# A hybrid block on one core: the recurrence's gates as pairs of 64-row matmuls, with the squares and some transposes in other slots

## The chip, the cores and the metric

The kernel runs on one core of one Trainium2 chip. The metric is the device time of one execution in microseconds. PE is TensorE, ACT ScalarE, DVE VectorE, POOL GpSimd, and SP the engine whose queue issues most DMAs.

## The reference

One block of a network over 512 tokens of 1024 features, in fp32: a norm, one input projection into seven parts, a gated linear recurrence and differential attention beside each other, a gated merge, an output projection with residual, a norm, an MLP and a last norm. What the change touches is the recurrence's gates (and the slots of the attention's steps):

```python
def rg_lru(x, w_a, b_a, w_x, b_x, lam):
    bsz, s, _ = x.shape
    xb = x.reshape(bsz, s, RNN_BLOCKS, RNN_BLOCK_W)
    r = jax.nn.sigmoid((jnp.einsum('bsni,nij->bsnj', xb, w_a) + b_a).astype(jnp.float32)).reshape(bsz, s, D_RNN)
    i = jax.nn.sigmoid((jnp.einsum('bsni,nij->bsnj', xb, w_x) + b_x).astype(jnp.float32)).reshape(bsz, s, D_RNN)
    log_a = -LRU_C * r * jax.nn.softplus(-lam.astype(jnp.float32))
    a = jnp.exp(log_a)
    mult = jnp.sqrt(-jnp.expm1(2.0 * log_a))
    u = mult * i * x.astype(jnp.float32)
...
    h = rms_norm(x, norm1_g[l])
    proj = h @ w_in[l]
    u_x, u_g, q, k, v, g_r, g_a = jnp.split(proj, cuts, axis=-1)
    xr = causal_depthwise_conv(u_x, conv_w[l], conv_b[l])
    y_rnn = rg_lru(xr, rg_a_w[l], rg_a_b[l], rg_x_w[l], rg_x_b[l], lru_lambda[l]) * jax.nn.gelu(u_g)
...
    y_attn = diff_attention(q, k, v, lam, lam_init, subln_g[l])
    merged = (jax.nn.sigmoid(g_r) * (y_rnn @ w_br_rnn[l])
              + jax.nn.sigmoid(g_a) * (y_attn @ w_br_attn[l]))
```

RNN_BLOCKS is 16 and RNN_BLOCK_W 64: each gate is sixteen products with a 64x64 matrix. There are 8 heads; a head has two maps of 64 features each.

## The kernel before, in words

Activations lie transposed, features on the 128 partitions and the 512 tokens along the free axis, in 8 tiles. Every fp32 product is split: each operand is a high part (hi, a cast to fp32r on ACT) and a rest (lo, a subtraction on DVE), and a product is three matmuls, hi by hi, hi by lo and lo by hi.

The first stage computes v; the norm's factors follow. The second, to which the change belongs, runs over 32 slots, j = 0 to 3 and n = 0 to 7 with s = 8j + n. Each slot issues one projection chunk of 24 matmuls of 128x128x512 (L166 to L168, output pmm). By n the chunk is q or k of head 2j (n = 0, 1), u_x (2, 3), q or k of head 2j + 1 (4, 5) or u_g (6, 7). Behind the chunk come the steps that `at(slot, f)` has placed there. For each head these are the scores in two halves (L544, pairs of matmuls of 64 rows; softmax on DVE and ACT, exponentials at L346), three groups of transposes of the probabilities (L582, copied out by ACT at L587 into pT or tmp), the product with v (`attn_out`, L598, copied out by ACT at L601 into Q) and the sums of squares of its output (`o_squares`, L608 on ACT). The table `sl` holds the slots of a head's steps, counted from its k chunk. At n = 5 come `lru_gates` and `lru_decay`, behind n = 7 the gelus of u_g, `lru_scan` (a square root on ACT, products and scans on DVE, L678 and L680) and `lru_out` (L683).

`lru_gates(j)` handles 256 features, as two tiles e of 128. For each e it loads a block-diagonal 128x128 matrix for each of the two gates (two 64x64 matrices on the diagonal), splits them (gwh on ACT, L654; gwl on DVE), and issues for each gate three matmuls of 128x128x512 (L659 to L661) into one half of a PSUM tile "sc" and a sigmoid of 128x512. The scores use the same two "sc" buffers.

The scheduler of the language decides the order of the instructions of each engine, within the dependences and the order in which the program is written. `act` chains the activations that need a table in the order of the program; `tc.keep_in_program_order` holds an instruction behind the one issued before it. `raw` are weights on arrival, `whi` and `wlo` their split (L136 and L137 by chunk, L204 and L205 by piece of the later units).

The third stage goes through units: "gr" (gate of the recurrence branch, sigmoid L346 into up or rot), "rnn" (branch matmuls on E and L), "ga", "att", "out", and the MLP's "one" and "two" (matmuls at L249). The last heads' scores, transposes, outputs and squares run between the first "gr" chunks, from slot 32 on.

Of the kernel before, what the change touches and what calls it, by code (L numbers as in the profile page):

```python
# [8 lines left out]
F = mybir.dt.float32  # L9
# [5 lines left out]
P = 128  # L15
# [5 lines left out]
NH = 8  # L21
# [275 lines left out]
def block_kernel(ctx: ExitStack, tc: tile.TileContext, a):  # L297
# [57 lines left out]
    def col(off, i):  # L355
        return sm[:, off + i:off + i + 1]
# [287 lines left out]
    def lru_gates(j):  # L644
        r_, i_, xr = lru_st[j][:3]
        xh_, xl_ = t("L3", (P, 2, T), FR), t(f"R{j}", (P, 2, T), FR)
        A.copy(xh_, xr)
        V.tensor_tensor(xl_, xr, xh_.bitcast(F), op=ALU.subtract)
        for e in range(2):
            m = 2 * j + e  # L650
            gw = t("tmp", (P, 2, P), bufs=2)
            nc.sync.dma_start(gw, a["gates"][m])
            gh, gl = t("gwh", (P, 2, P), FR), t("gwl", (P, 2, P), FR)
            A.copy(gh, gw)  # L654
            V.tensor_tensor(gl, gw, gh.bitcast(F), op=ALU.subtract)
            pgs = ps("sc", (P, 2, T), bufs=2)
            for g, dst, boff in ((0, r_, C_AB), (1, i_, C_XB)):
                pg = pgs[:, g]
                TE.matmul(pg, gh[:, g], xh_[:, e], start=True, stop=False)  # L659
                TE.matmul(pg, gh[:, g], xl_[:, e], start=False, stop=False)  # L660
                TE.matmul(pg, gl[:, g], xh_[:, e], start=False, stop=True)  # L661
                act(dst[:, e], pg, AF.Sigmoid, bias=col(boff, m))
        lru_st[j][3] = t("L3", (P, 2, T))

    def lru_decay(j):
# [28 lines left out]
    for j in range(KT // 2):  # L694
        for n in range(8):
            s = 8 * j + n
            p_ = b.proj(xh, xl)
            h = 2 * j + n // 4
            if n % 4 < 2:
                if n % 4 == 0:  # L700
                    qk = t(f"B{h % 2}", (P, 2, T))
                rope_load(p_, qk, n % 4)
                if n % 4 == 1:
                    qks = rope(h, qk)


                    sl = ((3, 6, 5, 8, 9, 10, 13), (4, 5, 6, 7, 8, 9, 12))[h % 2]
                    if h == NH - 1:
                        sl = (3, 4, 5, 6, 7, 8, 11)
                    for d, f, *args in zip(sl[2:], (attn_transpose,) * 3 + (attn_out, o_squares),  # L710
                                           (h,) * 5, ((0, 1), (2,), (3,), None, h + 1)):
                        at(s + d, f, *(x for x in args if x is not None))
                    at(s + sl[0], attn_scores, h, qks, 0)
                    at(s + sl[1], attn_scores, h, qks, 2)
            elif n < 4:
                lru_conv(j, n - 2, p_)
                if n == 3:
                    at(s + 2, lru_gates, j)
                    at(s + 2, lru_decay, j)
            else:  # L720
                if n == 6:
                    p_g = p_
                else:
                    yr[j] = t(f"R{j}", (P, 2, T))
                    act(yr[j][:, 0], p_g, AF.Gelu_apprx_tanh)
                    act(yr[j][:, 1], p_, AF.Gelu_apprx_tanh)
                    lru_scan(j)
                    lru_out(j)
            run(s)
# [239 lines left out]
def _layout(inputs):  # L969
# [20 lines left out]
        cols(g["rg_a_b"][0].reshape(-1)), cols(g["rg_x_b"][0].reshape(-1)), cols(g["lru_lambda"][0]),  # L990
        cols(g["conv_w"][0].reshape(-1)), cols(g["subln_g"][0]),
    ], axis=1)
    gates = np.zeros((KT, P, 2, P), np.float32)
    for s, n in ((0, "rg_a_w"), (1, "rg_x_w")):
        for blk in range(16):
            o = (blk % 2) * 64
            gates[blk // 2, o:o + 64, s, o:o + 64] = g[n][0, blk]
    half = HD // 2
    inv = np.float32(ROPE_THETA) ** (-np.arange(half, dtype=np.float32) * np.float32(2.0) / np.float32(HD))
    ang = np.arange(T, dtype=np.float32)[None, :] * inv[:, None].astype(np.float32)  # L1000
# [38 lines left out]
```

## Time and profile before

| | |
|---|---|
| median of 3 runs | 882.9 us (882.69 to 883.09) |
| profiled execution | 881.29 us, its span 879.5 us |
| granted TensorE clock, mean | 0.997 |
| busy PE, weight load, DVE, ACT | 867.0, 742.4, 623.1, 495.0 us |
| chain that ended last | PE 92%, ACT 3%, DVE 3% |

The table comes from the page of the profile: the busy time of an engine is the sum of its instructions, its share an average over all stages. The chain is followed back from the last instruction to what released it.

### The profile page before, as it was taken

The numbers are of one execution on the slowest core, as the hardware profiler recorded it, in microseconds if no ns is written. First come the engines' busy times: TensorE is split into PE (matmuls) and PEld (weight loads), VectorE is DVE, ScalarE is ACT, GpSimd is POOL, SyncE is SP. The second block draws the span as 40 slices with busy tenths as digits, with TensorE's granted clock in tenths as the row PEclk, the third lists the DMA queues.
The fourth block names the chain that finished last, engine by engine and source line by source line (L and its number), as shares of the span: only waits on it lengthen the run. The fifth ranks groups of instructions, "written<-read, shape, count | busy, mean of one in ns | idle before, by whom it ended". The sixth has DMA issues, their size and how long they took to land.

```text
span 879.5 us, 13019 instructions
## 1 busy us (share of the span) xinstructions
PE 867.0 (99%) x5033; PEld 742.4 (84%) x5033; DVE 623.1 (71%) x1071; ACT 495.0 (56%) x925; POOL 11.0 (1%) x17
## 2 busy tenths in 40 slices
PE   9999999999999999999999999999999999999996
PEld 7887788788788788889888889988888888888996
DVE  7777787795986866677765997766666666665533
ACT  7544856957868974544443555644444444444532
POOL 0000000000000012000000000000000000000000
PEclk9999999999999999999999999999999999999998
DMA  8433223134232257223225221222222222222211
GB/s 299 143 138 115 72 78 128 59 108 132 72 109 72 63 166 209 66 97 132 107 102 188 97 96 48 97 99 98 102 103 104 105 104 102 97 96 97 97 49 48
DMA packets 23917, 94.40 MB, mean 107 GB/s; under 512 B 3376, under 2 KB 6704, under 8 KB 14896
## 3 DMA queue, kind: packets, MB, share of 16 engines
q1 hardware_dynamic: 22128, 90.43, 29.7%
q0 software_dynamic: 1728, 3.15, 2.1%
q8 instruction: 39, 0.64, 0.3%
q14 instruction: 22, 0.18, 0.1%
HBM read 83.08 MB, written 2.10 MB: 97 GB/s over the span
## 4 chain that ended last, share of the span: by engine, by line
PE 92%; ACT 3%; DVE 3%; DMA 1%; issue 1%; SPq 0%; POOL 0%; DVEq 0%; ACTq 0%
PE pmm L249 38%; PE psc L249 22%; PE pmm L166 7%; PE pmm L167 7%; PE pmm L168 7%; PE pmm L454 3%; PE psc L454 3%; PE pmm L598 2%; PE psc L544 2%; DMA S<-X 1%; PE ptr L582 1%; ACT L346 1%; ACT L L346 1%; PE psc L659 0%; PE ptr L385 0%
## 5 line engine op out<-in xcount | busy, mean ns | idle before, releaser
L204 ACT CAST whi<-raw 128x512 fp32r<-128x512 f32 (+1 forms) x236 | 144.2, 627 | 207.5 <-PE pmm L249 103.9
L205 DVE TENSOR_TENSOR wlo<-raw,whi 128x512 fp32r<-128x512 f32 (+1 forms) x236 | 162.3, 697 | 48.0 <-ACT whi L204 44.7
L249 PE MATMUL psc<-X,whi 128*128 128x256 f32 x592 | 112.3, 288 | 0.6 <-DVE up L273 0.2
L249 PEld LDWEIGHTS psc<-X,whi 128*128 128x128 f32 x592 | 91.8, 189 | 8.1 <-DVE up L273 1.7
L249 PE MATMUL pmm<-E,whi 128*128 128x512 f32 x256 | 82.2, 397 | 0.3 <-ACT rot L346 0.3
L249 PE MATMUL psc<-X,wlo 128*128 128x256 f32 x296 | 81.1, 281 | 0.0
L166 PE MATMUL pmm<-X,whi 128*128 128x512 f32 x200 | 81.0, 405 | 0.0
L249 PE MATMUL pmm<-L,whi 128*128 128x512 f32 x256 | 80.6, 396 | 0.0
L167 PE MATMUL pmm<-X,whi 128*128 128x512 f32 x200 | 79.3, 397 | 0.0
L168 PE MATMUL pmm<-X,wlo 128*128 128x512 f32 x200 | 79.3, 396 | 0.0
L249 PE MATMUL psc<-Q,whi 128*128 128x256 f32 x320 | 70.2, 287 | 0.8 <-DVE tmp L269 0.8
L249 PEld LDWEIGHTS psc<-Q,whi 128*128 128x128 f32 x320 | 52.3, 188 | 6.4 <-DVE tmp L269 3.2
L249 PEld LDWEIGHTS pmm<-L,whi 128*128 128x128 f32 x256 | 48.1, 188 | 11.3
L249 PE MATMUL pmm<-B,whi 128*128 128x512 f32 (+1 forms) x224 | 57.6, 346 | 0.0
L249 PEld LDWEIGHTS pmm<-E,whi 128*128 128x128 f32 x256 | 47.7, 189 | 9.7 <-ACT rot L346 0.5
L249 PEld LDWEIGHTS psc<-X,wlo 128*128 128x128 f32 x296 | 55.0, 189 | 0.0
L249 PE MATMUL pmm<-V,whi 128*128 128x512 f32 (+1 forms) x192 | 53.2, 357 | 0.0
L249 PE MATMUL pmm<-L,wlo 128*128 128x512 f32 x128 | 50.8, 397 | 0.0
L249 PE MATMUL pmm<-E,wlo 128*128 128x512 f32 x128 | 50.7, 396 | 0.0
L136 ACT CAST whi<-raw 128x1024 fp32r<-128x1024 f32 (+1 forms) x36 | 34.3, 955 | 27.4 <-PE pmm L167 22.0
L166 PEld LDWEIGHTS pmm<-X,whi 128*128 128x128 f32 x200 | 37.7, 189 | 10.4 <-issue 1.5
L137 DVE TENSOR_TENSOR wlo<-raw,whi 128x1024 fp32r<-128x1024 f32 (+1 forms) x36 | 39.3, 1099 | 8.8 <-ACT whi L136 8.8
(312 smaller groups left out, 1873.5 us busy)
## 6 DMA issues: line engine op xcount, KB each, us to landing
raw<-wts SPq DMA_DIRECT2D x70, 1024.0 KB, 4.8
rot<-B SPq DMA_DIRECT2D x64, 64.0 KB, 2.0
L<-xT SPq DMA_DIRECT2D x8, 256.0 KB, 5.3
raw<-wts SPq DMA_DIRECT2D x8, 256.0 KB, 5.3
S<-X SPq DMA_DIRECT2D x8, 256.0 KB, 2.8
S<-X POOLq DMA_DIRECT2D x8, 256.0 KB, 4.4
R<-xT SPq DMA_DIRECT2D x8, 256.0 KB, 4.6
out<-R SPq DMA_DIRECT2D x6, 256.0 KB, 2.5
```

Source lines behind the costliest of these rows:

```text
L136: nc.scalar.copy(hf[:, s], raw[:, s])
L137: nc.vector.tensor_tensor(lf[:, s], raw[:, s], hf[:, s].bitcast(F), op=ALU.subtract)
L166: nc.tensor.matmul(ps, hi[:, k], xh[k], start=(k == 0), stop=False)
L167: nc.tensor.matmul(ps, hi[:, k], xl[k], start=False, stop=False)
L168: nc.tensor.matmul(ps, lo[:, k], xh[k], start=False, stop=(k == KT - 1))
L204: self.nc.scalar.copy(hi, src)
L205: self.nc.vector.tensor_tensor(lo, src, hi.bitcast(F), op=ALU.subtract)
L249: nc.tensor.matmul(out, l[:, k], r, start=((first if clear is None else clear) and k == 0 and g == 0), stop=(last and k == 3 and g == 2), ...
L346: ins = A.activation(*args, **kw).ins
L454: TE.matmul(pvs[half][i], xs[q][:, i * P:(i + 1) * P], (hv, lv)[wi][:, q % 2], start=(q == 0 and n == 0), stop=(q == KT - 1 and n == 2))
L544: ins = TE.matmul(scs[i - i0][:, m, :n], l[rows, 0, i * P:n], r[rows, 1, :n], start=(g == 0), stop=(g == len(terms_) - 1))
L598: TE.matmul(po[:, i], pdT[:, j], v[j][:, h * P:(h + 1) * P], start=(j == 0), stop=(j == i))
```

## The change

It does four things. (1) The gates of one j are one transfer and one split instead of two: the host lays the matrices out so that the 64 rows of a 64x64 block hold both gates' matrices side by side, 64 columns each. (2) The matmuls use 64 rows each: for each e and each of the three products a pair, one on the upper and one on the lower half of the rows, each with 128 columns of which 64 belong to each gate; both e follow one another without another matmul between, and hold both "sc" buffers. Twelve matmuls per j, as before. (3) The result of a pair's half c has one gate on partitions 0 to 63 and the other on 64 to 127, the other way round for c = 1. So the sigmoids take 64 rows each: eight of 64x512 for each j in place of four of 128x512; those of the second gate read from one half of the partitions and write to the other. (4) In the table of slots the squares of the even heads come one slot earlier and those of the odd ones two later; for heads 4 to 6 they come at slots 33 to 35. An odd head's first transposes and second group come one slot later.

```diff
+        gw = t("tmp", (P, 2, P), bufs=2)
+        nc.sync.dma_start(gw, a["gates"][j])
+        gh, gl = t("gwh", (P, 2, P), FR), t("gwl", (P, 2, P), FR)
+        A.copy(gh, gw)
+        V.tensor_tensor(gl, gw, gh.bitcast(F), op=ALU.subtract)
+        pgs = [ps("sc", (P, 2, T), bufs=2) for _ in range(2)]
+        first = True
         for e in range(2):
-            m = 2 * j + e
-            gw = t("tmp", (P, 2, P), bufs=2)
-            nc.sync.dma_start(gw, a["gates"][m])
-            gh, gl = t("gwh", (P, 2, P), FR), t("gwl", (P, 2, P), FR)
-            A.copy(gh, gw)
-            V.tensor_tensor(gl, gw, gh.bitcast(F), op=ALU.subtract)
-            pgs = ps("sc", (P, 2, T), bufs=2)
-            for g, dst, boff in ((0, r_, C_AB), (1, i_, C_XB)):
-                pg = pgs[:, g]
-                TE.matmul(pg, gh[:, g], xh_[:, e], start=True, stop=False)
-                TE.matmul(pg, gh[:, g], xl_[:, e], start=False, stop=False)
-                TE.matmul(pg, gl[:, g], xh_[:, e], start=False, stop=True)
-                act(dst[:, e], pg, AF.Sigmoid, bias=col(boff, m))
+            for g, (l, r) in enumerate(((gh, xh_), (gh, xl_), (gl, xh_))):
+                for c in range(2):
+                    rows = slice(c * HD, (c + 1) * HD)
+                    ins = TE.matmul(pgs[e][:, c], l[rows, e], r[rows, e], start=(g == 0), stop=(g == 2))
+                    if not first:
+                        tc.keep_in_program_order(ins)
+                    first = False
+        for e in range(2):
+            for dst, boff, flip in ((r_, C_AB, 0), (i_, C_XB, 1)):
+                for c in range(2):
+                    to, of = (slice(x * HD, (x + 1) * HD) for x in (c, c ^ flip))
+                    act(dst[to, e], pgs[e][of, c], AF.Sigmoid, bias=col(boff, 2 * j + e)[to])
...
-                    sl = ((3, 6, 5, 8, 9, 10, 13), (4, 5, 6, 7, 8, 9, 12))[h % 2]
+                    sl = ((3, 6, 5, 8, 9, 10, 12), (4, 5, 7, 8, 8, 9, 14))[h % 2]
                     if h == NH - 1:
                         sl = (3, 4, 5, 6, 7, 8, 11)
+                    if 4 <= h < NH - 1:
+
+                        sl = sl[:6] + (8 * NH // 2 + h - 3 - s,)
...
-    gates = np.zeros((KT, P, 2, P), np.float32)
+    gates = np.zeros((KT // 2, P, 2, 2, HD), np.float32)
     for s, n in ((0, "rg_a_w"), (1, "rg_x_w")):
         for blk in range(16):
             o = (blk % 2) * 64
-            gates[blk // 2, o:o + 64, s, o:o + 64] = g[n][0, blk]
+            gates[blk // 4, o:o + 64, blk // 2 % 2, s ^ (blk % 2)] = g[n][0, blk]
+    gates = gates.reshape(KT // 2, P, 2, P)
```

The order on ACT in the second block of gates (j = 1), before. `gwh` is the cast of the gates' matrices, `psc` the gates' PSUM, `L` the gates r and i, `S` the split of head 3's q and k, `Q` the output of a head; the squares are the L608 rows:

```order
L136 CAST whi_1436<-raw_1378 128x1024
L654 CAST gwh_1357<-tmp_1355 128x256
L346 ACTIVATE L_203_1112<-psc_1346,small_61 128x512
L524 CAST S_243_1325<-B_227_1242 128x1024
L346 ACTIVATE L_202_1111<-psc_1361,small_61 128x512
L608 ACTIVATE tmp_1410,ss_544<-Q_220_1203,r_101_543 128x128
L608 ACTIVATE tmp_1412,ss_544<-Q_220_1203,r_101_543 128x128
L608 ACTIVATE tmp_1414,ss_544<-Q_220_1203,r_101_543 128x128
L346 ACTIVATE L_203_1112<-psc_1361,small_61 128x512
L346 ACT_TABLE_LOAD
L346 ACTIVATE L_257_1370<-L_202_1111,cneg_536 128x512
```

The same place after the change:

```order
L136 CAST whi_1432<-raw_1383 128x1024
L652 CAST gwh_1349<-tmp_1347 128x256
L524 CAST S_239_1318<-B_222_1234 128x1024
L346 ACT_TABLE_LOAD
L346 ACTIVATE L_199_1109<-psc_1353,small_61 64x512 x2
L346 ACTIVATE L_200_1110<-psc_1353,small_61 64x512 x2
L346 ACTIVATE L_199_1109<-psc_1354,small_61 64x512 x2
L346 ACTIVATE L_200_1110<-psc_1354,small_61 64x512 x2
L346 ACT_TABLE_LOAD
L346 ACTIVATE L_255_1375<-L_199_1109,cneg_536 128x512
L601 COPY Q_217_1201<-pmm_1414 128x512
```

All sigmoids of the block now stand behind the cast of S and the table load, and the squares are gone from between them.

The order on PE where the last heads' steps end and the first branch matmuls begin, before. `ptr` are transposes of probabilities, V the values, pT and tmp the copied transposes, E the operand of the branch matmuls; the place is behind the last "gr" chunk:

```order
L598 MATMUL pmm_2866<-V_39_137,pT_2542 128x128
L598 MATMUL pmm_2866<-V_37_135,tmp_2827 128x128
L598 MATMUL pmm_2866<-V_38_136,tmp_2827 128x128
L598 MATMUL pmm_2866<-V_39_137,tmp_2827 128x128
L598 MATMUL pmm_2866<-V_40_138,tmp_2827 128x128
L582 MATMUL ptr_2879<-ident_108,B_535_2777 128x128 x3
L598 MATMUL pmm_2891<-V_37_135,pT_2833 128x128 x2
L598 MATMUL pmm_2891<-V_38_136,pT_2833 128x128
L249 MATMUL pmm_2930<-E_515_2686,whi_2390 128x512 x2
L249 MATMUL pmm_2930<-E_515_2686,wlo_2391 128x512
L249 MATMUL pmm_2930<-E_516_2689,whi_2390 128x512
L582 MATMUL ptr_2884<-ident_108,B_535_2777 128x128 x4
```

The same place after the change:

```order
L598 MATMUL pmm_2858<-V_39_137,pT_2525 128x128
L582 MATMUL ptr_2821<-ident_108,B_495_2657 128x128 x3
L598 MATMUL pmm_2858<-V_37_135,tmp_2819 128x128
L598 MATMUL pmm_2858<-V_38_136,tmp_2819 128x128
L598 MATMUL pmm_2858<-V_39_137,tmp_2819 128x128
L598 MATMUL pmm_2858<-V_40_138,tmp_2819 128x128
L582 MATMUL ptr_2880<-ident_108,B_519_2760 128x128 x3
L598 MATMUL pmm_2892<-V_37_135,pT_2825 128x128 x2
L598 MATMUL pmm_2892<-V_38_136,pT_2825 128x128
L249 MATMUL pmm_2922<-E_499_2669,whi_2379 128x512 x2
L582 MATMUL ptr_2885<-ident_108,B_519_2760 128x128 x4
```

The last head's first transposes (`ptr_2821`) have come out of the last "gr" chunk to this place, and two branch matmuls in place of four stand ahead of its last transposes.

## Rows read from the trace of the kernel before

**Rows 1.** The page, part 1: busy time, share of the span and instructions.
```profile
PE 867.0 (99%) x5033; PEld 742.4 (84%) x5033; DVE 623.1 (71%) x1071; ACT 495.0 (56%) x925; POOL 11.0 (1%) x17
```

**Rows 2.** Busy time in windows: PE, PEld, DVE, ACT, POOL; clock; DMA.
```profile
280.00:300.00 20.00, 19.32 (x99) 14.17 (x99) 17.35 (x34) 19.14 (x37) 0.00 (x0) 1.00 0.03 10
300.00:320.00 20.00, 19.54 (x111) 16.22 (x110) 11.07 (x21) 19.85 (x52) 3.65 (x4) 1.00 0.74 207
```

**Rows 3.** Timeline of PE, first block: start, duration, engine, line, operation.
```profile
90.32 0.50 PE L659 MATMUL psc<-L,gwh 128*128 128x512 f32 x1
90.65 0.39 PE L660 MATMUL psc<-R,gwh 128*128 128x512 f32 x1
```

**Rows 4.** Timeline of PE: pairs of 64-row matmuls of the scores.
```profile
101.15 0.39 PE L168 MATMUL pmm<-X,wlo 128*128 128x512 f32 x1
101.47 0.44 PE L544 MATMUL psc<-E 64*128 64x384 f32 x2
101.75 0.51 PE L544 MATMUL psc<-E,E 64*128 64x384 f32 x4
102.10 0.39 PE L544 MATMUL psc<-E 64*128 64x512 f32 x2
102.33 0.63 PE L544 MATMUL psc<-E,E 64*128 64x512 f32 x4
102.89 0.50 PE L166 MATMUL pmm<-X,whi 128*128 128x512 f32 x1
103.23 0.39 PE L167 MATMUL pmm<-X,whi 128*128 128x512 f32 x1
```

**Rows 5.** Groups by line and form on ACT: the gates' sigmoids (busy, mean ns).
```profile
L346 ACT ACTIVATE L<-psc,small 128x512 f32<-128x512 f32 x16 | 11.0, 686 | 4.3 <-PE psc L661 4.2
```

**Rows 6.** Timeline of ACT, second block; in brackets the idle time ahead.
```profile
151.68 0.41 ACT L654 CAST gwh<-tmp 128x256 fp32r<-128x256 f32 x1
...
153.48 1.05 ACT L524 CAST S<-B 128x1024 fp32r<-128x1024 f32 x1 [0.81 <-DVE B L521]
154.50 0.69 ACT L346 ACTIVATE L<-psc,small 128x512 f32<-128x512 f32 x1
155.09 0.39 ACT L608 ACTIVATE tmp<-Q,r 128x128 f32<-128x128 f32 x1
...
157.06 1.28 ACT L346 ACT_TABLE_LOAD   x1
158.35 0.72 ACT L346 ACTIVATE L<-L,cneg 128x512 f32<-128x512 f32 x1
```

**Rows 7.** Timeline of ACT: an exponential of 128 columns.
```profile
295.54 0.37 ACT L346 ACTIVATE B<-psc,nb 128x128 f32<-128x128 f32 x1
```

**Rows 8.** Timeline of ACT, fourth block.
```profile
269.47 1.14 ACT L204 CAST whi<-raw 128x512 fp32r<-128x512 f32 x2 [1.41 <-PE pmm L167]
...
274.51 0.67 ACT L346 ACTIVATE L<-psc,small 128x512 f32<-128x512 f32 x1
```

**Rows 9.** Timeline of PE, second block: gates, next chunk, transposes of the even head.
```profile
148.01 0.39 PE L659 MATMUL psc<-L,gwh 128*128 128x512 f32 x1
...
162.36 0.50 PE L166 MATMUL pmm<-X,E 128*128 128x512 f32 x1
...
173.57 0.49 PE L582 MATMUL ptr<-ident,B 128*128 128x128 f32 x3
```

**Rows 10.** Timeline of DVE, second block.
```profile
167.03 1.23 DVE L678 TENSOR_TENSOR L<-L,L 128x1024 f32<-128x1024 f32 x1 [1.24 <-ACT L L346]
...
172.28 1.28 DVE L571 SCALAR_TENSOR_TENSOR B<-up,cf,B 128x384 f32<-128x384 f32 x2
```

**Rows 11.** Timeline of ACT, first block: first and last of four sigmoids.
```profile
89.58 0.69 ACT L346 ACTIVATE L<-psc,small 128x512 f32<-128x512 f32 x1
...
94.28 0.69 ACT L346 ACTIVATE L<-psc,small 128x512 f32<-128x512 f32 x1 [1.05 <-PE psc L661]
```

**Rows 12.** Timeline of PE at the first branch matmuls.
```profile
313.44 0.74 PE L249 MATMUL pmm<-E,whi 128*128 128x512 f32 x2 [0.32 <-ACT rot L346]
```

## The prediction

> **What bounds the kernel now.** I read the page first: TensorE (PE) is busy 867.0 of 879.5 us, 99% [rows 1], so at first sight every microsecond of matmul that goes is a microsecond of time. That share is an average, and the change lies in four places (four blocks, one for each j) between 82 and 320 us. So next I read the windows: between 280 and 320 us ScalarE (ACT) is busy 19.14 and 19.85 us of 20, while PE loses 0.68 and 0.46 us [rows 2]. Ahead of the end of this stage ACT has no time left and PE is the one that waits: an ACT chain that gets longer there is paid in full. Then the timelines of PE and ACT around a block say how long the removed matmuls take and who waits for what.
>
> The profiled execution took 881.29 us, a span of 879.5 and 1.79 around it; the median of the three runs is 882.9, so the profile stands 1.6 us (0.18%) under it. I add what follows to the median. A measurement of this kernel can tell about 0.2% from no change, 1.8 us.
>
> **PE: the gates' matmuls.** Before, a block issues twelve 128-row matmuls of 512 columns, one every 0.23 us, and loses time where they follow other shapes: 90.32 to 90.65 is 0.33 instead of 0.23 [rows 3]; all such steps of the first block make 0.41. 12 x 0.229 + 0.41 = 3.16 us. The new form, 64-row pairs that run at the same time, has its model in the scores, which use the same pairs [rows 4]: 102.10 to 102.33 is 0.23 for a pair of 512 columns, as long as one matmul of 128 rows. Entering costs 0.09 (101.15 to 101.47 is 0.32), the first pair 0.10 more than the next (0.28 for 384 columns against half of 0.35), leaving 0.10 (102.33 to 102.89 is 0.56 for two pairs) and the matmul behind it 0.11 (102.89 to 103.23 is 0.34). Six pairs in a row: 6 x 0.23 + 0.38 to 0.40 = **1.76 us**. So PE has less work by 3.16 - 1.76 = 1.40 in block 1; in blocks 2 to 4, where the twelve cost 3.0 to 3.2, by about 1.25 each. Together 5.2 us: the most that the change can give.
>
> The trace shows that pairs cost an entry and an exit. The Trainium skill (TensorEngine Tiling (Array Packing), Key Properties) states that changing the tiling mode drains TensorE, and it agrees; the same page (PSUM Bottleneck) says that tiling speeds up TensorE but not the evacuation of PSUM, and advises to use VectorE too. That is a rule against this change as written, since all eight sigmoids of a block stay on ACT.
>
> **ACT: the sigmoids.** Before, four of 128x512 per block, 686 ns each [rows 5], 0.59 from start to start (154.50 to 155.09 [rows 6]). After, eight of 64x512. The trace has no 64-row instruction on ACT, so I bound its price: below by half, 0.30, if time went with all elements; above by 0.59, the same. An exponential of 128 columns takes 0.37 and the sigmoid of 512 columns 0.69 [rows 6, 7]: time goes with the free size, and that stays 512. I take **0.59**; four more cost 2.36 per block, and one of two casts of the gates (0.41 [rows 6]) goes.
>
> The Trainium skill (ScalarE: Activation LUTs, What ACT_TABLE_LOAD costs) says 280 ns + 0.833 ns per column, one element per cycle in each lane: 706 ns for 512 columns, whatever the rows; the 686 of the trace agree, and no run here shows 64 rows. By it the sum is the same.
>
> More than the 2.36 matters where they stand. Before, the sigmoids were spread among the matmuls, and ACT did the table load and the first of them in its gaps (0.81 idle ahead of 153.48 even so [rows 6]; 1.41 ahead of 269.47 [rows 8]). After, the order shows all eight behind the cast of S, which waits for DVE at 153.48, and behind the table load.
>
> - Block 2 (block 3 repeats it). Cast S 153.48, sigmoid table at 154.50, first sigmoid at 155.78, eight by 0.59 end at 160.6; before, the exp table followed at 157.06 [rows 6]. Chain +3.5; one square (0.39) leaves it: the square root behind it ends at 170.2 instead of 167.0.
> - What this holds up, first: the next chunk takes the PSUM bank of attn_out, so PE waits for the copy of Q. After the sigmoids come table 1.28, one exponential 0.72 [rows 6], the copy, some 0.5: it ends at 163.1. PE started that chunk at 162.36 [rows 9] and, 0.56 faster by the new matmuls (1.25 less the 0.69 below), would want it at 161.8. The gain is gone and 0.7 more.
> - Second: DVE's products and scans of the recurrence start at 167.03 on that square root, and the combination of the softmax (L571) is behind them; its first half ends at 172.9 [rows 10], 5.9 behind the root. PE transposes it at 173.57 [rows 9], with only 0.7 to spare. After: wanted at 163.1 + 11.2 = 174.3, there at 170.2 + 5.9 = 176.1. PE stands **2.5 us** later than before at this place. Of it the three matmuls at 148.01 [rows 9], now behind that chunk, give back 0.69 ahead of it; DVE has one split of gates less ahead of 153.48, for which I take off 0.2. Net **+1.6** each for blocks 2 and 3, +3.2.
> - Block 1: there no cast stands ahead of the sigmoids. The four began at 89.58 and, each waiting for its matmuls, ended at 94.97 [rows 11]; eight in a row from 89.58 end at 94.4. Nothing comes later, so I keep the whole **-1.4**. If the chain came as in block 2, it would be up to +1.6.
> - Block 4: -0.7 for the group ahead of the chunk's end. Then ACT: from 269.47 (a wait for the chunk's end [rows 8]) two casts 1.14, cast of gates 0.4, two squares 0.78, cast S 1.05, table 1.28, eight sigmoids 4.72: 278.8, where the last sigmoid ended at 275.2 before [rows 8]. +3.6. From there to 313 ACT is full but for some 1.0 us [rows 2], of which I let 0.5 be taken up: **+3.1** at the second gate sigmoid, for which PE waited already (0.32 ahead of 313.44 [rows 12]).
> - The end of the stage. The new order has the last head's first transposes behind the last gate chunk, where they were inside it, and on ACT the copies of pT behind two casts and a copy of Q. PE may wait 2.1 us more for them, or, if it finds other work, 0. I take the middle, **+1.0**.
>
> **Edits with one answer.** The gates' four transfers fewer on SP (and their splits on DVE) land long before they are used: nothing. The squares' slots: they change places on ACT, their number is the same; what left blocks 2 and 3 is counted, and in the slots where they go (19, 21, 27) ACT has idle time that hides them; without that cover each 0.39. The odd heads' later first transposes leave PE its number of transposes, and give the softmax a slot (5.5 us) more: counted at 0, below by what they save, the 0.2 to 0.5 us waits of such places; above 0.
>
> **Sum:** -1.4 + 3.2 - 0.7 + 3.1 + 1.0 = +5.2 us: 882.9 + 5.2 = **888.1 us**, slower by 0.6%.
>
> **The rivals.**
> 1. The slack is larger than I count, and ACT bites only in block 4: -1.4 - 2.5 - 0.7 + 3.1 + 0 to 1.0 = -1.5 to -0.5: about 881.9. For it: 0.7 of slack is a small number out of a long chain, and the scheduler has moved the odd heads' transposes too. Against: the head that waits here is the even one, whose slots stay. It decides if the root ends within 0.7 us of its time of before.
> 2. 64-row sigmoids take half the time: eight end 2.4 us earlier, the root stands +0.8 in blocks 2 and 3 and is covered, block 4 pays 1.2 with PE's gain kept ahead: -1.4 - 2.5 - 0.7 + 1.7 = -2.9: 880.0. Against: 0.37 for 128 columns, 0.69 for 512 [rows 6, 7].
> 3. **Faster, the other side:** ACT has no deadline at all in these blocks, because PE, where it waits, has the 32-slot stage's other matmuls, and what it loses at one place it gains at the next. Then PE's work alone decides: -5.2, 877.7. For it: over the span PE idles 1% [rows 1], and the wait of 0.32 us is small [rows 12]. Against: an in-order PE cannot pass over the transposes that wait. It decides if no idle time of PE above 0.3 us stands behind blocks 2 to 4.
> 4. The pairs do not overlap (the change does not do what it says): twelve at 0.23 + 0.38, no gain on PE: block 1 gives 0, the ACT-bound rest stays: 889.5. Against: the scores' pairs, with the same shape of tiles, do overlap [rows 4].
>
> **How the numbers follow.** Forecast 0.47, rival 1 0.18 (half of it faster, half of it no change), rival 2 0.12, rival 3 0.15, rival 4 0.08. Faster by over 0.2%: 0.15 + 0.12 + 0.07 = 0.34. Within 0.2%: 0.11 of rival 1 and 0.01 of the forecast: 0.12. Slower: 0.54. The forecast's own range goes from 884.5 (blocks 2 and 3 at 0.3 each, end at 0) to 890.2 (end at 2.1, block 4 at 3.6, blocks at 1.8). Both signs hold much of the chance: from 878.0, which leaves out half of rival 3, to 890.0, which leaves out some 0.1 above.
>
> **What would show it.** Right: in the profile after, a sigmoid of 64x512 of about 690 ns and eight in a row; the six pairs in 1.8 us; PE idle some 0.7 us on the copy of Q and 1 to 2 us on the transposes after blocks 2 and 3; ACT without gaps to the second gate sigmoid, that sigmoid 4 to 5 us later than before. Wrong: sigmoids of 0.4 us; no idle of PE at these places; ACT idle between 280 and 310 us; the first branch matmuls at the same distance from the last gate sigmoid as before.

## The result and the profile after

The changed kernel takes 894.76 us (median of 4 runs, 893.38 to 895.43) beside 882.8 us before (882.61 to 883.09): ratio 1.0132, 95% interval 1.0118 to 1.0145. It is slower by 12.0 us, in the direction of the forecast and more than twice its +5.2. The profiled execution took 895.43 us with a span of 893.7.

The page after the change: busy times, the clock by slices, and the chain that ended last by engine.

```profile
PE 868.9 (97%) x5033; PEld 740.7 (83%) x5033; DVE 618.9 (69%) x1067; ACT 505.7 (57%) x937; POOL 11.0 (1%) x17
...
PEclk9999999999999989999999999999999999999998
...
PE 81%; ACT 11%; DVE 4%; DMA 2%; issue 1%; SPq 0%; DVEq 0%; ACTq 0%
```

ACT does 10.7 us more than before [rows 1] and holds 11% of the chain, where it held 3%. One slice ahead of the last shows a granted clock of 0.8, where before none did (the last shows it in both). Windows tell where the time went, first of the kernel before, then after (columns: PE, PEld, DVE, ACT, POOL busy; granted clock; DMA share; GB/s).

```profile
60.00:140.00 80.00, 80.00 (x390) 63.56 (x389) 61.96 (x98) 48.02 (x82) 0.00 (x0) 1.00 0.31 100
140.00:200.00 60.00, 60.00 (x312) 48.55 (x311) 47.58 (x77) 43.91 (x91) 0.00 (x0) 1.00 0.29 94
200.00:260.00 60.00, 60.00 (x313) 48.59 (x312) 47.28 (x79) 44.64 (x96) 0.00 (x0) 1.00 0.29 94
260.00:300.00 40.00, 39.33 (x198) 30.53 (x197) 29.12 (x52) 35.04 (x71) 0.00 (x0) 1.00 0.22 72
300.00:345.00 45.00, 44.54 (x226) 36.60 (x225) 32.96 (x60) 30.46 (x68) 8.03 (x9) 1.00 0.65 173
```

```profile
60.00:140.00 80.00, 79.75 (x392) 63.08 (x392) 62.10 (x97) 52.10 (x93) 0.00 (x0) 1.00 0.31 101
140.00:200.00 60.00, 56.93 (x288) 45.37 (x287) 43.34 (x70) 44.58 (x91) 0.00 (x0) 0.97 0.28 88
200.00:260.00 60.00, 56.97 (x302) 45.17 (x301) 44.15 (x71) 44.43 (x87) 0.00 (x0) 1.00 0.27 83
260.00:300.00 40.00, 37.66 (x200) 29.37 (x198) 25.15 (x42) 31.64 (x58) 0.00 (x0) 1.00 0.24 81
300.00:345.00 45.00, 40.35 (x199) 32.58 (x198) 30.73 (x66) 35.91 (x85) 5.38 (x6) 0.92 0.45 117
```

From 60 to 345 us PE idles 13.3 us (0.25 + 3.07 + 3.03 + 2.34 + 4.65), where it idled 1.1: 12.2 more. The granted clock loses another 5.1: in windows of 5 us it is 0.75 and 0.90 from 175 to 185 us, 0.59 and 0.73 from 320 to 330 us, and 1.00 in all others of this stretch. With the 5.2 us of matmul time that the prediction counted as gained, 12.2 + 5.1 - 5.2 = 12.1. The medians differ by 12.0. The two profiled executions differ by more, 14.2 us of span; some 1.0 of it stands ahead of the first block already (the projection's first matmul comes at 52.23 us before and at 53.27 after), which leaves 13.1 for these 12.1. So the gain on PE is there, and more than three times as much is lost to waits and clock.

The timeline of PE after: the gates of the second block, and each wait of more than 0.6 us (in brackets, with what ended it).

```profile
151.53 0.50 PE L662 MATMUL psc<-L,gwh 64*128 64x512 f32 x2
151.86 0.39 PE L662 MATMUL psc<-R,gwh 64*128 64x512 f32 x2
...
152.80 0.39 PE L662 MATMUL psc<-L,gwl 64*128 64x512 f32 x2
153.11 1.16 PE L598 MATMUL pmm<-V,tmp 128*128 128x128 f32 x8
...
163.02 0.50 PE L166 MATMUL pmm<-X,E 128*128 128x512 f32 x1 [1.38 <-ACT Q L601]
...
176.10 0.52 PE L582 MATMUL ptr<-ident,B 128*128 128x128 f32 x3 [1.68 <-DVE B L571]
...
226.24 0.51 PE L166 MATMUL pmm<-X,whi 128*128 128x512 f32 x1 [1.36 <-ACT Q L601]
...
239.32 0.52 PE L582 MATMUL ptr<-ident,B 128*128 128x128 f32 x3 [1.56 <-DVE B L571]
...
288.23 0.73 PE L249 MATMUL pmm<-X,whi 128*128 128x512 f32 x2 [1.39 <-ACT Q L601]
...
297.87 0.49 PE L544 MATMUL psc<-B 64*128 64x128 f32 x4 [0.94 <-ACT up L346]
...
322.45 0.90 PE L582 MATMUL ptr<-ident,B 128*128 128x128 f32 x3 [4.29 <-ACT tmp L587]
```

The pairs run as forecast: one every 0.23 us, 1.58 us from the first pair to the matmul behind them; with 0.09 for the entry and 0.11 for the matmul behind, as in [rows 4], that is 1.78, beside the 1.76 forecast. Three waits are for the copy of Q, two for L571, one for an exponential (into up) and one for the copy of the last transposes. The sigmoids, by form:

```profile
L346 ACT ACTIVATE L<-psc,small 64x512 f32<-64x512 f32 x32 | 21.9, 683 | 0.5
```

683 ns for 64 rows, against 686 for 128 [rows 5]. But in a row the 64-row ones start 0.70 us apart, as a run below shows against 128-row ones.

### The profile page after: what moved, and what is told of

It reads as the page before. It is cut to its first block, busy times and chain, and to the rows that moved or that the text cites. A ratio compares the mean times of both kernels' runs of the same rounds, so it can differ in the third digit from the quotient of the medians.

```text
span 893.7 us, 13008 instructions
## 1 busy us (share of the span) xinstructions
PE 868.9 (97%) x5033; PEld 740.7 (83%) x5033; DVE 618.9 (69%) x1067; ACT 505.7 (57%) x937; POOL 11.0 (1%) x17
## 4 chain that ended last, share of the span: by engine, by line
PE 81%; ACT 11%; DVE 4%; DMA 2%; issue 1%; SPq 0%; DVEq 0%; ACTq 0%
PE pmm L249 38%; PE psc L249 22%; PE pmm L166 4%; PE pmm L167 4%; PE pmm L168 4%; ACT L L346 4%; ACT L346 2%; PE psc L454 2%; PE pmm L454 2%; PE pmm L598 1%; DMA raw<-wts 1%; PE psc L544 1%; PE ptr L582 1%; DMA L<-xT 1%; ACT up L346 1%
## 5 line engine op out<-in xcount | busy, mean ns | idle before, releaser
L168 PEld LDWEIGHTS pmm<-X,wlo 128*128 128x128 f32 x200 | 38.1, 190 | 9.2
```

Source lines behind the costliest of these rows:

```text
L168: nc.tensor.matmul(ps, lo[:, k], xh[k], start=False, stop=(k == KT - 1))
```

## Experiments

Theory A is the forecast's: the four extra sigmoids of a block, and where they stand, make the ACT chain late. Theory B: the table of slots, which I had costed at 0, costs time of its own. Later a theory C joined: the gates' transfer comes late because it shares a buffer. Each run is compared with the kernel before on the same chip (medians 882.7, 882.25, 882.53, 882.29 and 882.66 in the five groups, in the order in which they ran).

### The two halves of the change, and four sigmoids

**Gates only**: the new gates with the old table.

```diff
-                    sl = ((3, 6, 5, 8, 9, 10, 12), (4, 5, 7, 8, 8, 9, 14))[h % 2]
+                    sl = ((3, 6, 5, 8, 9, 10, 13), (4, 5, 6, 7, 8, 9, 12))[h % 2]
...
-                    if 4 <= h < NH - 1:
...
-                        sl = sl[:6] + (8 * NH // 2 + h - 3 - s,)
```

> The new gates (pairs, eight 64x512 sigmoids) with the slot table of before. Theory A (the time goes to the sigmoids: eight at full price in a row push ACT's chain back, and PE waits behind blocks 2 to 4 for the copy of Q, the combination of the softmax and, at the end, the copy into tmp): still slower than before by 6 to 14 us, 889 to 897 us, with waits of PE of over 1 us behind each of blocks 2 to 4. Rival B (the slot table is what costs: squares and an odd head's transposes in worse slots): within 2 us of before or faster, 878 to 885 us.

**Slots only**: the reverse, the old `lru_gates` and matrices with the new table.

> The gates of before with the new slot table. Theory A: the table alone moves work that has cover: 882 to 885 us, no wait of PE over 1 us between 60 and 340 us. Rival B: most of the 12 us is here: 890 us or more.

**Four sigmoids** on the whole change:

```diff
-            for dst, boff, flip in ((r_, C_AB, 0), (i_, C_XB, 1)):
-                for c in range(2):
-                    to, of = (slice(x * HD, (x + 1) * HD) for x in (c, c ^ flip))
-                    act(dst[to, e], pgs[e][of, c], AF.Sigmoid, bias=col(boff, 2 * j + e)[to])
+            for c, (dst, boff) in enumerate(((r_, C_AB), (i_, C_XB))):
+                act(dst[:, e], pgs[e][:, c], AF.Sigmoid, bias=col(boff, 2 * j + e))
```

> The change with four sigmoids of 128x512 per block in place of eight of 64x512, nothing else touched. It leaves out the sorting of the two gates onto their partitions, so the recurrence gets mixed gates. Theory A: ACT has 2.4 us less in each block, so the three waits for the copy of Q (1.5 us each) and the two for the softmax (1.8 us each) go or shrink below 0.5, the wait at the end (4.5 us) shrinks by over 2, and the clock stays at 2.4 GHz: 880 to 885 us. Rival B, or rival C (it is the bunching behind the cast of S and the table load, not the number of sigmoids): at least half of the loss stays, 888 us or more.

Measured: gates only 888.68 us (1.0073, 1.0056 to 1.0091), slots only 892.16 (1.0110, 1.0095 to 1.0125), four sigmoids 882.98 (1.0004, 0.9995 to 1.0014). The gates alone cost 6.0 us, close to the 5.2 that the prediction had for the whole. The table alone costs 9.5, where theory A expected 882 to 885 us. They don't add: together 12.0. With four sigmoids in place of eight (that kernel leaves the two gates mixed on their partitions), gates and table together take as long as the kernel before. Its ACT has the change's order in block 2, with the transfer as late (146.65 us) and the sigmoids in a row behind the cast of S and the table load:

```profile
153.79 2.43 ACT L346 ACTIVATE L<-psc,small 128x512 f32<-128x512 f32 x4
```

Four take 2.43 us, one every 0.57 to 0.59, where the change's eight take 5.58 (154.88 in its timeline below), one every 0.70. So it is their number and this distance that cost there, not that they stand in a row. Why 64-row ones follow one another more slowly is not settled. But the 5.2 us of PE don't show either: PE still waits 0.59, 0.73, 1.60, 0.36 and 1.95 us. And the table costs 9.5 with the old gates, whose sigmoids are four. So neither theory has the whole: both the table and the four extra sigmoids are in the loss.

SP's queue (issue of the gates' transfer of the second block) shows what the table does; before, then after:

```profile
141.58 0.40 SPq L652 DMA_DIRECT2D tmp<-gates  x1
```

```profile
145.22 2.41 SPq L515 DMA_DIRECT2D rot<-B  x4
147.72 0.53 SPq L650 DMA_DIRECT2D tmp<-gates  x1
```

And ACT's timeline there, before, then after:

```profile
146.29 0.41 ACT L654 CAST gwh<-tmp 128x256 fp32r<-128x256 f32 x1 [0.46 <-DMA tmp<-gates]
146.71 1.28 ACT L346 ACT_TABLE_LOAD   x1
148.91 0.69 ACT L346 ACTIVATE L<-psc,small 128x512 f32<-128x512 f32 x1 [0.91 <-PE psc L661]
```

```profile
150.07 1.04 ACT L136 CAST whi<-raw 128x1024 fp32r<-128x1024 f32 x1 [3.11 <-PE pmm L167]
151.02 0.40 ACT L652 CAST gwh<-tmp 128x256 fp32r<-128x256 f32 x1
152.51 1.05 ACT L524 CAST S<-B 128x1024 fp32r<-128x1024 f32 x1 [1.09 <-DVE B L521]
153.59 1.28 ACT L346 ACT_TABLE_LOAD   x1
154.88 5.58 ACT L346 ACTIVATE L<-psc,small 64x512 f32<-64x512 f32 x8
```

The transfer is issued 6.1 us later than before, behind four others. It starts some 0.1 us after them, so at this point its place in SP's queue holds it back, not a wait of its own. The cast of the gates now stands behind a cast of weights that waits for the end of the chunk, with ACT idle for 3.11 us ahead of it; the first sigmoid starts at 154.88 instead of 148.91. In "gates only" the transfer was issued at 142.21 and the first sigmoid started at 151.15; in "slots only" 148.57 and 153.59, and its second cast of gates stands at 156.76 between the sigmoids, which still waited for their matmuls up to 160.24. The gates' matrices share the two buffers named "tmp" with the copies of the transposes and the squares, whose slots the table moves: the even head's squares now come in the slot of `lru_gates`, and ACT starts them at 135.14 us, ahead of the transfer, where before they started at 155.09, behind it. Which of the moved rows makes the transfer late was not tried one by one.

### Moving the copy of Q to DVE

```diff
-        A.copy(o_raw[h // 2][:, h % 2], po.rearrange("p a c -> p (a c)"))
+        V.tensor_copy(o_raw[h // 2][:, h % 2], po.rearrange("p a c -> p (a c)"))
```

> The change with the copy of attn_out's result (Q) on VectorE instead of ScalarE. Theory A: PE's three waits for this copy behind blocks 2 to 4 go (4.6 us together), and ACT's chain is 0.5 us shorter per block; the wait for the softmax's combination stays and takes back up to 1.5 us in blocks 2 and 3, so 889 to 892 us. If the waits only move on to the next place that hangs on the same ACT chain: 893 to 896 us.

Measured: 900.2 us (1.0204, 1.0184 to 1.0225), where 889 to 896 was expected. The waits for Q are gone, but the waits for L571 grow to 2.64 each. The windows of this kernel from 140 us on:

```profile
140.00:200.00 60.00, 57.04 (x286) 45.21 (x285) 44.49 (x72) 43.74 (x89) 0.00 (x0) 0.97 0.28 88
200.00:260.00 60.00, 57.18 (x290) 45.21 (x289) 42.46 (x69) 41.26 (x78) 0.00 (x0) 0.94 0.24 75
260.00:300.00 40.00, 38.46 (x198) 30.22 (x196) 26.08 (x46) 31.14 (x57) 0.00 (x0) 1.00 0.27 93
300.00:345.00 45.00, 39.27 (x186) 31.94 (x187) 28.77 (x61) 35.52 (x88) 4.53 (x5) 0.85 0.40 105
```

PE idles 13.3 us as in the change itself, 0.27 of it ahead of 140 us. What differs is the clock: in windows of 5 us it loses 12.0 us instead of 5.1, and the kernel is 5.4 us slower than the change. The wait for L571, which hangs on the same chain (sigmoids, square root, products), took over what the wait for Q gave back. The waits are fewer and longer than the change's; whether that is why the clock falls more is not settled.

### The first block alone

The old kernel with the new gates for j = 0 only (`if j == 0:` around the new code, `else:` the old).

> The kernel before, its slot table too, with the new gates in block 1 (j = 0) alone. Theory A: in block 1 the new matmuls give 1.4 us and nothing is late behind them: 881.0 to 881.8 us against 882.7. Rival B' (any change of the gates puts the scheduler's order out and costs later): 883 us or more.

Measured: 881.63 us (0.9992, 0.9983 to 1.0001). In the profile the chunk behind the block starts 1.41 us earlier, counted from the chunk ahead of the block, as forecast (1.40). Some 30 us on 0.6 of it is lost again: the matmuls of the next scores start further apart, and the chunk behind them comes only 0.8 earlier. The 0.6 us that show at the end can't be told from no change.

### Fewer table loads

If ACT's chain binds, eight table loads fewer (1.28 us each) should give much of the time back. Sigmoid is (1 + tanh(x/2))/2, and tanh lies in the same table as the exponential (before, ACT goes from the exponential at 158.35 us to the tanh at 159.37 without a table load); the halves go into `cneg`, `cpos`, one product and the scale of the square root.

```diff
-    V.tensor_scalar(cneg, z2, -8.0, None, op0=ALU.mult)
-    V.tensor_scalar(cpos, z2, 8.0, None, op0=ALU.mult)
+    V.tensor_scalar(cneg, z2, -4.0, None, op0=ALU.mult)
+    V.tensor_scalar(cpos, z2, 4.0, None, op0=ALU.mult)
...
-                    act(dst[to, e], pgs[e][of, c], AF.Sigmoid, bias=col(boff, 2 * j + e)[to])
+                    act(dst[to, e], pgs[e][of, c], AF.Tanh, scale=0.5,
+                        bias=hb[to, boff - C_AB + 2 * j + e:boff - C_AB + 2 * j + e + 1])
```

On the change:

> The change, all eight 64x512 activations kept, but each gate as half of 1 + tanh of half its argument: tanh lies in the table of exp, so of the five table loads of 1.28 us in each block two go (the halves are folded into the scales and biases of what follows). Theory A (what counts is the length of ACT's chain ahead of the copy of Q, the square root and the exponentials, whatever it consists of): 2.56 us less per block does what four sigmoids less did (883.0): 878 to 884 us, PE's waits for Q under 0.5 us each. Rival C (eight half-height reads in a row, or half-height writes across the partitions, cost by themselves): 888 us or more.

On the new gates with the old table:

> The new gates with the slot table of before and with the gates by tanh as in the run before. The new gates with the old table had 888.7 us. Theory A: two table loads less per block take 5 to 9 us off: 880 to 884 us. If the slot table does its part only with the new gates, then this is slower than the change with tanh by 1 us or more; else it is the faster of the two.

On the kernel before:

> The kernel before with the gates by tanh. Theory A: the kernel before loses only some 2 us to ACT between 60 and 330 us, so 2.56 us less per block can give no more than that: 880.5 to 882.9 us. If ACT's chain bounded the whole kernel before as well, it would be 875 us or less.

Measured, each beside the kernel before of its own group: on the change 886.75 us (1.0051, 1.0036 to 1.0066), 7.5 us less than without tanh, but above the 878 to 884 expected; on the gates alone 884.38 (1.0025, 1.0013 to 1.0037), 3.9 less (6.0 to 2.1 above before); on the kernel before 886.73 (1.0050, 1.0035 to 1.0065), 4.5 us **more**, where 0 to 2 less was expected. The traces have 23 table loads where there were 31. DVE's timeline of that last kernel, and PE's, show what took the place:

```profile
312.24 0.69 DVE L284 TENSOR_TENSOR S<-S 128x512 f32<-128x512 f32 x1 [6.77 <-DMA S<-X]
```

```profile
315.06 0.52 PE L584 MATMUL ptr<-ident,B 128*128 128x128 f32 x3 [2.71 <-DVE B L573]
```

DVE has the combination of the gate branch (L284) in its queue ahead of the last head's softmax (L571 of the kernel before, L573 here), and idles 6.77 us for the transfer that it needs. The softmax stands behind it, and PE waits for it. It could have run some 5 us earlier: in the run below in which it does not stand behind L284, its first step starts at 308.41 us, here at 313.77. "Slots only" shows the same: DVE idle 5.57 us at L284, then PE:

```profile
320.88 0.87 PE L582 MATMUL ptr<-ident,B 128*128 128x128 f32 x3 [4.04 <-DVE B L571]
```

### Taking the softmax out from behind the transfer

First bluntly: the first subtraction of the combination is held in the order of the program, which moves many other instructions too.

```diff
-        V.tensor_tensor(tt[:, 0:3:2], q4[:, 0:2], q4[:, 1:4:2], op=ALU.subtract)
+        ins = V.tensor_tensor(tt[:, 0:3:2], q4[:, 0:2], q4[:, 1:4:2], op=ALU.subtract)
+        if hold:
+            self.tc.keep_in_program_order(ins)
```

On the old table with tanh, the table alone, and the kernel before with tanh:

> The new gates by tanh with the slot table of before (884.4 us), and on VectorE the first subtraction of the gate branch's combination held behind what the program issues before it. In that run VectorE sat 7.0 us in its queue on this subtraction, whose transfer had not landed, with the last head's softmax behind it, and PE waited 2.8 us for that. Theory A2 (the last of the loss is an order on VectorE that the scheduler made, not ScalarE): that wait goes below 0.5 us, 880.5 to 882.5 us. Rival (ScalarE's chain ends there just as late): the wait stays above 1.5 us and the time above 883.5 us.

> The gates of before with the new slot table (892.2 us), and the same subtraction held. There VectorE sat 5.6 us on it and PE waited 4.25 us, about half of what the table cost. Theory A2: 887 to 889.5 us, the waits of 1.5 us each behind blocks 2 and 3 stay. Rival (the wait at the end is of ScalarE's making): 891 us or more.

> The kernel before with the gates by tanh (886.7 us), and the same subtraction held. There PE waited 2.9 us for the softmax behind it. Theory A2: all that tanh lost goes, since it was this order and not the table loads: 880 to 883 us. Rival: 885 us or more.

Measured: 888.11 us (1.0055), 895.3 (1.0141), 886.34 (1.0039), all three above what was expected. In the first the wait at 314 us is gone, but PE waits 3.2 us at 347.31 for the merge (V, L366). In the second the wait of 4.04 us is down to 1.64, but new ones of 1.95, 1.02 and 1.25 us stand at 367.57, 376.38 and 380.16. In the third new waits of 0.61, 1.01 and 1.19 us stand at 345.64, 352.86 and 366.28.

Then with one dependence alone: that subtraction after the last softmax combination (`add_manual_dep`), which puts the three instructions of the combination (L284 and the two behind it) after the softmax.

> As the run with the new gates by tanh and the slot table of before (884.4 us), but the gate branch's first subtraction on VectorE waits only for the last head's softmax combination, not for all that the program issues before it; no other instruction of VectorE changes its place. Theory A2 (VectorE's queue stood behind a transfer that had not landed, the last softmax behind it): PE's wait of 2.8 us at 314 us goes, and nothing new comes at 347 us as with the stricter hold: 880.5 to 882.5 us. Rival: the wait stays over 1.5 us, 883.5 us or more.

> The kernel before with the gates by tanh (886.7 us), with the same single dependence. Theory A2: the loss of 4 us was this order alone; without it two table loads less per block give what the kernel before loses to ScalarE, 0 to 2 us: 880.5 to 882.5 us. Rival: 885 us or more.

> The change with tanh (886.8 us), its own slot table, with the same dependence. There VectorE sat only 1.2 us on the subtraction and PE waited 1.7 us for ScalarE's copy into tmp: Theory A: little to gain, 885 to 887.5 us, since what is left is ScalarE's chain (2.8 us of wait at 289 us and a low clock behind it). Rival (the order on VectorE is the last of the loss in every kernel): 883.5 us or less.

Measured: old table with tanh 881.89 us (0.9998, 0.9987 to 1.0010), 2.5 less; before with tanh 883.46 (1.0006, 0.9998 to 1.0015), 3.3 less, though above the 880.5 to 882.5 expected; the change with tanh 887.19 (1.0055, 1.0042 to 1.0067), no gain. DVE's timeline of the first (L577 is the softmax there):

```profile
307.47 1.28 DVE L577 SCALAR_TENSOR_TENSOR B<-up,cf,B 128x384 f32<-128x384 f32 x2
...
312.02 0.69 DVE L284 TENSOR_TENSOR S<-S 128x512 f32<-128x512 f32 x1 [3.27 <-DMA S<-X]
```

The softmax is done 3 us before the transfer lands, and PE waits for it no more; what is left there is 1.01 us for ACT's copy into tmp. (The profiled execution is one of 885.82 us, 3.9 above the median; PE waits 1.94 and 1.38 us at 352.83 and 366.47 in it, places that the dependence does not touch.) So the wait of PE for the softmax at the end of the stage is DVE's order, in those kernels that have it. The change with tanh has the order too, but DVE stands only 1.23 us at L284, and the softmax behind it then still waits 0.54 us for ACT's exponentials: with the dependence it starts at 312.34 us, without it at 312.64.

### The gates' transfer ahead of its buffer

Theory C by itself: the gates' matrices land in a part of the tiles for r and i that is written later, not in "tmp".

```diff
-        gw = t("tmp", (P, 2, P), bufs=2)
+        gw = i_[:, 1, :2 * P].rearrange("p (a c) -> p a c", a=2)
```

On the table alone (there in r and i in turn), on the change, on the old table with tanh and the dependence, and on the change with both:

> The gates of before with the new slot table (892.2 us); the gates' matrices land in the half of the gate tiles that their own last sigmoid fills later, and no longer in the two tmp buffers that they share with the transposes and the squares. With the table their transfer was issued at 148.6 us in place of 141.6, so the cast stood behind the weight cast that waits for the chunk's end at 150.9. Theory D (that is what the table costs): the first sigmoid of block 2 comes 3 us or more earlier, the waits of 1.5 us behind blocks 2 and 3 go: 883 to 888 us. Rival (the later transposes and squares cost by themselves): 891 us or more.

> The change with its own sigmoids and slots, the gates' matrices landing in the gate tile as in the run before this. Theory D: with the eight sigmoids in the gap that ACT had ahead of the chunk's end, the waits for Q and the softmax behind blocks 2 to 4 go below 0.5 us, and the clock stays at 2.4 GHz; of 12 us most comes back and the gain on PE shows: 878 to 884 us. Rival (the eight sigmoids are too many wherever they stand): 889 us or more.

> The new gates by tanh, slot table of before, softmax ahead of the subtraction (881.9 us), and the gates' matrices landing in the gate tile. With the old table their transfer was early already: Theory D: no more than 1 us, 880 to 882 us. If ScalarE's chain gets shorter here as well: 877 to 880 us.

> The change's slot table, tanh, softmax ahead of the subtraction (887.2 us), and the gates' matrices landing in the gate tile: everything that the runs found, together. Theory D: the waits of 0.8 to 1.0 us behind blocks 2 and 3 and of 2.8 us in block 4 go: 877 to 882 us, the fastest of all; beyond 884 us theory D falls for this table.

Measured: the table alone 882.06 us (0.9996, 0.9987 to 1.0005), 10.1 less than with "tmp", each beside the kernel before of its own group; the change 883.92 (1.0020, 1.0009 to 1.0031), 10.7 less; 881.28 (0.9987, 0.9978 to 0.9995); and 880.96 (0.9984, 0.9975 to 0.9992). ACT's timeline of the change with the early transfer:

```profile
145.30 1.28 ACT L346 ACT_TABLE_LOAD   x1
146.59 0.68 ACT L346 ACTIVATE L<-psc,small 64x512 f32<-64x512 f32 x1
...
147.77 4.89 ACT L346 ACTIVATE L<-psc,small 64x512 f32<-64x512 f32 x7
```

The eight sigmoids end at 152.66, ahead of where the change's first one starts. Behind blocks 2 and 3 no wait above 0.6 us is left, the clock stays at 1.00, and the two longest waits left are 1.65 us at 288.53 and the one of DVE's order:

```profile
311.79 0.69 DVE L284 TENSOR_TENSOR S<-S 128x512 f32<-128x512 f32 x1 [7.97 <-DMA S<-X]
```

```profile
314.61 0.52 PE L582 MATMUL ptr<-ident,B 128*128 128x128 f32 x3 [2.28 <-DVE B L571]
```

So the table costs through the late transfer: with the same table and the transfer early nothing of the 9.5 us is left. And eight sigmoids that start early leave the change 1.3 us over the kernel before. So late transfer and eight sigmoids lose the 12.0 us together: an early transfer brings back 10.7 of them, four sigmoids 11.7. That the shared buffer is what makes it late is shown in so far as another place ends it; the move also takes the gates' tiles out of the ring for everyone else, and which of the two the scheduler answers to is open. The last kernel, the change with all three mends, has the lowest median: 0.16% under the kernel before (interval 0.08 to 0.25%), a small difference, and 1.5% under the change. Between it and the one ahead of it (0.13% under) the runs do not tell.

## Why the prediction was right or wrong

**Right.** A 64-row sigmoid costs no less than one of 128 rows, so rival 2 falls. The pairs overlap, rival 4 falls. Block 1 gives 1.41 (forecast 1.40), of which 0.6 goes again later. In blocks 2 and 3 the waits came where the prediction put them. Ahead of block 2 the two traces stand 0.14 us apart:

```profile
143.14 0.39 PE L166 MATMUL pmm<-X,whi 128*128 128x512 f32 x1
```

```profile
143.00 0.39 PE L166 MATMUL pmm<-X,whi 128*128 128x512 f32 x1
```

From there the eight sigmoids end at 160.46 (forecast 160.6), the chunk behind the copy of Q starts at 163.02 (163.1) and the transposes behind L571 at 176.10 (176.1). PE waited 1.38 and 1.36 us for the copy of Q, for the 1.3 that 163.1 - 161.8 makes (the signs of the prediction call it 0.7, which is how much later the chunk starts), and 1.68 and 1.56 for L571, for the 1.8 that 176.1 - 174.3 makes. That the dates agree so well is in part luck: the first sigmoid starts 0.9 earlier than forecast (154.88 for 155.78), and the eight take 5.58 us where 0.59 each made 4.8. Rivals 1 and 3 asked for no such waits. The four extra sigmoids are one of the two causes, as four in their place bring 883.0. The Trainium skill (TensorEngine Tiling (Array Packing), PSUM Bottleneck) says that tiling speeds up TensorE and not the evacuation of PSUM. The trace agrees: the pairs take 1.78 us where the twelve matmuls took 3.16, while eight sigmoids take 5.58 where four take 2.43.

**Wrong, first: the clock**, which the sum did not contain: 5.1 us after, none before in this stretch, in two places that follow waits. It is most of the miss. Windows of after:

```profile
178.00:181.00 3.00, 3.00 (x8) 2.32 (x8) 2.98 (x6) 0.12 (x1) 0.00 (x0) 0.51 0.40 96
...
322.00:324.00 2.00, 1.55 (x8) 1.55 (x8) 1.05 (x2) 2.00 (x5) 1.05 (x2) 0.50 0.30 113
```

0.51 and 0.50 are the lower of the two levels, 1.2 GHz.

**Second: what was taken off in blocks 2 and 3.** The prediction found PE 2.5 us later at the transposes, took off 0.69 and 0.2 and kept 1.6 for each block. Counted from the chunks ahead of the blocks, PE stands 2.7 and 2.6 us later there. The wait ends when DVE is done, and DVE when ACT is; what PE had saved ahead of it (the 0.69) only made it wait longer. For block 2 that is 173.57 and 176.10 with the 0.14 of above, for block 3 233.11 and 239.32 at the transposes, and 202.59 and 206.25 at the chunk ahead.

**Third: block 4 and the end of the stage.** The sum had 3.1 and 1.0. From the last chunk of the projection (274.32 us before, 279.70 after) to the fourth branch matmul on L (324.99 and 338.83) 8.5 us are lost, 3.4 of them to the clock and 5.1 otherwise. The price of a sigmoid, 0.59 from start to start, was too low by 0.11, which makes 0.8 for the eight of this block (in blocks 2 and 3 their earlier start hid it). The copy of Q cost 1.39 in block 4, for which the sum had nothing, and the last transposes waited 4.29, where 0 to 2.1 was forecast. The second gate sigmoid on ACT came 10.5 us later, where the forecast had 4 to 5; before, then after:

```profile
312.78 0.61 ACT L346 ACTIVATE rot<-pmm 128x512 f32<-128x512 f32 x1
```

```profile
319.65 1.28 ACT L346 ACT_TABLE_LOAD   x1
320.94 0.60 ACT L346 ACTIVATE rot<-pmm 128x512 f32<-128x512 f32 x1
...
321.82 0.57 ACT L587 COPY tmp<-ptr 128x512 f32<-128x512 f32 x1
...
323.33 0.60 ACT L346 ACTIVATE rot<-pmm 128x512 f32<-128x512 f32 x1
```

The copy into tmp, for which PE waited, stands behind a gate's sigmoid, its table load and everything that was late. Together the three make 8.2 us: 5.1 for the clock, 2.1 in blocks 2 and 3 (2.7 + 2.6 for twice 1.6) and 1.0 here (5.1 for 4.1). The traces lie 7.9 over the sum (13.1 - 5.2).

**Fourth: the table of slots**, a wrong cause more than a wrong number. "The squares' slots: they change places on ACT, their number is the same ... counted at 0." I looked for what the squares cost, not for what they share. The table alone costs 9.5 us with the old gates, and 6.0 on top of the new ones (12.0 - 6.0). The sum did hold the late sigmoids of blocks 2 and 3, since I read their place off the order after the change. But I did not ask why they stood so late, nor date the cast of the gates one row above them anew, nor the transfer that it waits for, which comes 6.1 us later. With the transfer early all eight sigmoids stay and the change costs 1.3 us.

The top of the forecast's own range adds up to 890.1, not 890.2.

## What to carry to other kernels

A table of slots moves more than the work it names: whatever shares a buffer with that work (here a transfer of 128 KB) can be issued later, so look up in the new order where each transfer of the affected buffers is issued, on its queue, before a row is costed at 0. When work is split into smaller pieces for one engine, count the pieces of the engine that empties its results, by free size and not by rows. When a wait ends with another engine's work, what is saved ahead of it is not gained: here 0.69 us of matmuls moved ahead of a wait and the wait took them. When an engine waits at the end, look for what stands ahead of the late instruction on its queue: one dependence that moved three instructions gave 2.5 and 3.3 us in the two kernels whose softmax stood ready behind them and nothing in a third; a hold that moved many gave 0.7 us in one kernel and cost over 3 in two.

## What had not been expected of the hardware

After PE's idle time of 1.68 us ahead of 176.10 the granted clock fell to half for some 3.5 us; after 1.56 us ahead of 239.32 it did not, nor in another kernel after 2.28 us ahead of 314.61. With the same idle time of 13.3 us, one kernel lost 5.1 us to the clock and another 12.0. Which waits bring it down these runs do not settle; the fall behind the wait of 1.68 us cost 1.7, as much again.

Sigmoids of 64x512 in a row start 0.70 us apart in all four blocks of the change, those of 128x512 in the kernel with four 0.57 to 0.59 apart, though one of either takes 0.68 to 0.69 us.
